# Tile-wise waits between pools, even gate steps, and low one-hot products on GpSimd in a PEER transformer layer

## The chip, the cores and the metric

The kernel runs on one core of a Trainium2 chip. The metric is the device time of one execution in microseconds (us). Before the change three runs took 3026.48, 3026.91 and 3030.73 us; the median is 3026.91. One execution was profiled, and all durations below come from its trace.

The engines are called by the trace's short names too: PE is TensorE (matrix products), DVE is VectorE, ACT is ScalarE, POOL is GpSimd and SP is SyncE, which here only issues DMAs.

## What is computed

The reference is one layer of a diffusion transformer for 1024 tokens of width 1024, with a final norm. First comes a block of windowed attention, a short convolution and a gated merge. Then comes the PEER block, a layer of 16,384 experts, each a vector u and a vector v. Each token picks 16 experts for each of 8 heads:

```
s      = einsum(query, sub_keys)                  # 128 scores for each of 2 key halves
best   = top 16 of (top 16 of s[0]) + (top 16 of s[1])
g      = softmax(best)                            # gates, 8 heads x 16
act    = gelu(u[idx] . token)
out    = sum over the 128 picks of g * act * v[idx]
```

The kernel computes this block in two ways. For the first 512 tokens (the first half, `hf = 0`) and for 384 of the second 512 it takes the dense way: all experts are applied to all tokens as large matrix products, and a gate matrix G (experts x tokens, zero where an expert was not picked) multiplies gelu(u . token) or, for those 384, the stored product. For the second half the values gelu(u . token) come from gathered rows of u, and the last 128 tokens also gather their rows of v.

To keep fp32 accuracy, operands are split into a high and a low fp16 part, and a product is three products: high x high, high x low, low x high.

## The kernel before, in words

The gate matrix is built in tiles of 128 tokens. `select` (line 839) is one tile's top-k work on VectorE. `build_g` (965) then makes G for the tile. It goes through 16 groups of 8 tokens. For each group it makes four tiles of 128x1024 fp16 on VectorE: `e1`, a one-hot of the first expert index; `ah` and `al`, e1 times the high and the low part of the gate; and `e2`, a one-hot of the second index. Each is a product of two tiles in SBUF, with step-0 broadcasts. `expand` (997) multiplies e2 with ah and with al on TensorE into PSUM; ScalarE copies the result to a tile `ge`, and after two groups a DMA stores ge to the DRAM tensor `gd`: from GpSimd's queue in the first half, from ScalarE's in the second. A group is expanded one group after its tiles were made. e1 has one buffer; ah, al and e2 have two. `gates(0)` (1011) runs select and build_g for the four tiles of the first half while `stage2(1)` (718) runs the merge and the query projections of the second half. `gates_stream` (1043) does the same for the second half while the experts run.

Work of two kinds is interleaved when the program is written. `run_side` (1059) takes a main generator (which yields at each step) and a gates generator. After each main step it adds credit for gate steps, `grate` times the TensorE time that a simple model gives to that main step, and takes a gate step for each whole unit of credit. `GATES_B = 0.64` is the rate beside stage2(1), `GATES_D = 0.072` beside the experts. Before tile (1, 0) has been selected, credit is 1 per main step. The gathered rows have a rate of their own. A gates generator that has to wait (for the dot products of its tile) yields False; then the loop ends and the credit stays. When the main steps are over, gate steps that are left run at once. VectorE's order is tied to this order: a gate step's VectorE instructions stand behind the main step's last one. GpSimd and SyncE each run their own instructions in order.

`experts` (1386) drives the dense stage. For the first half there are 128 slots (`slot_dense`, 1158), one for each block of 128 experts: 24 matrix products with u (`ups`), gelu, the gate product, the split into `wdh` and `wdl`, and two of the eight output blocks of the previous group of four slots (`res`, `vps`, 12 products each). 376 main steps make up the first half. The second half (`slot_mix`, 1199) loads gates from gd again (`gt`), and its first load needs all of the second half's gd. Around slot 0 three u products with early weights (`u_first`, made in the pool `wts`) run first, and the slots 0 to 2 read gelu values from DRAM (`gel<-ged`).

Memory is handed out by pools that are opened and closed like a stack on two sides of SBUF. In this kernel a pool that lands on the bytes of closed pools waits, with all its tiles, for every user of those pools. The pools of the dense stage (`acc`, `dense0`, `gate1`, and `psV` in PSUM) are opened after `wts`, `gate0`, both `half` pools, `s2` and `x1` have been closed (lines 1408 to 1475).

Of the kernel before, what the change touches and what calls it, by code (L numbers as in the profile page):

```python
# [11 lines left out]
F16 = mybir.dt.float16  # L12
# [6 lines left out]
PSUM = bass.MemoryType.PSUM  # L19

D = 1024
# [8 lines left out]
TB = 8  # L30
REP = 4
NDENSE = 512
NMIX = 384
LATE_DOTS = 34
GATES_B = 0.64
GATES_D = 0.072
AHEAD = 1
GR = 8
GATE_AT = (2, 5)
# [3 lines left out]
SUB = 4  # L43
# [79 lines left out]
class K:  # L123
# [9 lines left out]
        self.waiting = []  # L133
        self.turned = None

    def pool(self, name, side=None, space=None, bufs=1):
        kw = {}
        if side is not None:
            kw["side"] = side
        if space is not None:  # L140
            kw["space"] = space
        g = self.tc.tile_pool(name=name, bufs=bufs, **kw)
        p = g.__enter__()
        return g, p
# [820 lines left out]
    def build_g(self, t, hf):  # L965

        nc, p = self.nc, self.pg
        yield
        yield
        ii, g16 = self.slots(t, hf)  # L970
        yield
        late = []
        for q in range(128 // 16):
            ge = p.tile([128, 128, 16], F32, name="ge", tag="ge", bufs=self.ge_bufs)
            for sub in range(16 // TB):
                t0 = q * 16 + sub * TB
                ts = slice(t0, t0 + TB)

                def onehot(name, src, idx, op):
                    x = p.tile([128, TB, 128 // REP, REP], F16, name=name, tag=name, bufs=1 if name == "e1" else 2)  # L980
                    nc.vector.tensor_tensor(x, src, idx[:, ts].unsqueeze(2).to_broadcast([128, TB, 128 // REP, REP]),
                                            op=op)
                    return x

                e1 = onehot("e1", self.iota, ii[:, 0], ALU.is_equal)
                ah = onehot("ah", e1, g16[:, 0], ALU.mult)
                al = onehot("al", e1, g16[:, 1], ALU.mult)
                e2 = onehot("e2", self.iota, ii[:, 1], ALU.is_equal)
                late.append((t, hf, q, sub, ge, ah, al, e2))
                if len(late) > 1:  # L990
                    self.expand(*late.pop(0))
                yield
        for x in late:
            self.expand(*x)
            yield
# [20 lines left out]
    def open_gate(self, name, side, ge_bufs):  # L1016
        nc, a = self.nc, self.a
        self.ge_bufs = ge_bufs
        g, self.pg = self.pool(name, side=side)
        p = self.pg  # L1020
        io32 = p.tile([128, 128], F32, name="io32", tag="dot", bufs=1)
        nc.sync.dma_start(io32, a["iota"])
        io16 = p.tile([128, 128], F16, name="iotas")
        nc.vector.tensor_copy(io16, io32)
        self.iota = io16.rearrange("p (a b) -> p a b", b=REP).unsqueeze(1).to_broadcast([128, TB, 128 // REP, REP])
        self.cand = p.tile([128, 8, NCAND], F32, name="cand", tag="cand", bufs=1)
        nc.vector.memset(self.cand[:, :, 16:128], NEG)
        self.iota16 = p.tile([128, 16, 16], F16, name="iota16")
        nc.vector.tensor_copy(self.iota16, io32[:, 0:16].unsqueeze(2).to_broadcast([128, 16, 16]))
        return g  # L1030
# [28 lines left out]
    def run_side(self, main, gates=None, grate=0.0, rows=None, rate=0.0, first=None):  # L1059


        pe, dve = self.nc.tensor, self.nc.vector
        last = pe.spent
        due = gdue = 0.0
        alive = gates is not None
        for _ in main:
            spent = pe.spent - last
            with nullcontext() if dve.pin else self.tc.issue_after(dve.last):
                due += rate
                while due >= 1.0:  # L1070
                    due -= 1.0
                    if next(rows, False) is False:
                        due = 0.0
                gdue += 1.0 if first is not None and first not in self.sel else grate * spent
                while alive and gdue >= 1.0:
                    r = next(gates, StopIteration)
                    alive = r is not StopIteration
                    if r is False:
                        break
                    gdue -= 1.0  # L1080
            last = pe.spent
        if alive:
            for _ in gates:
                pass
# [50 lines left out]
    def split_v(self, i1, v32, p):  # L1135
        if v32 is None:
            return self.vparts[i1]
        vh = p.tile([128, D], F16, name="vh", tag="vh", bufs=2 * SUB)
        vl = p.tile([128, D], F16, name="vl", tag="vl", bufs=2 * SUB)
        self.nc.scalar.activation(vh, v32, AF.Copy, scale=16.0)  # L1140
        self.late[0].append((vl, v32, 16.0, vh))
        if i1 >= 128 - 2 * SUB:
            self.vparts[i1] = vh, vl
        return vh, vl
# [13 lines left out]
    def slot_dense(self, i1, p, pv, outs):  # L1158
        nc = self.nc
        nb = NDENSE // 32  # L1160
        hh, hl = self.h2h[0], self.h2l[0]
        self.load_u(i1 + 2, p)
        v32 = self.load_v(0, i1, p)
        self.block_gates(0, i1, p)
        wh = self.pac.tile([128, NDENSE], F16, name="wdh", tag="wdh", bufs=2 * SUB)
        wl = p.tile([128, NDENSE], F16, name="wdl", tag="wdl", bufs=2 * SUB)
        ge = p.tile([128, NDENSE], F32, name="gel", tag="gel", bufs=2)
        if i1 < UPRE:
            nc.sync.dma_start(ge, self.ged[i1])
        else:  # L1170
            uh, ul = self.uparts.pop(i1)
            ps = pv.tile([128, 512], F32, name="ups", tag="v", bufs=3)
            for k in range(8):
                self.mm3(ps, uh[:, k, :], ul[:, k, :], hh[:, k, :], hl[:, k, :], k == 0, k == 7)
        self.lows(1)
        self.lows(0)
        if outs:
            yield 0
        if i1 >= UPRE:
            nc.scalar.activation(ge, ps, AF.Gelu, scale=2.0 ** -12)  # L1180
        self.split_u(i1 + 2, p)
        vh, vl = self.split_v(i1, v32, p)
        ends = []
        for k, out in enumerate(outs):
            ends.append(out())
            if k == 0:
                yield 0
        for end in ends:
            end()
        gev = ge.rearrange("p (b t) -> p b t", t=16)  # L1190
        for q in range(2):
            qs = slice(nb * q, nb * q + nb)
            nc.vector.tensor_mul(gev[:, qs, :], gev[:, qs, :], self.gts[q][:, :, i1 % GR, :])
        nc.scalar.activation(wh, ge, AF.Copy, scale=256.0)
        self.late[0].insert(0, (wl, ge, 256.0, wh))
        yield 0
        return vh, vl, wh, wl

    def slot_mix(self, i1, p, outs):
        nc = self.nc  # L1200
        nb = NMIX // 32
        v32 = self.load_v(1, i1, p)
        self.block_gates(1, i1, p)
        self.lows(0)
        vh, vl = self.split_v(i1, v32, p)
        wh = self.pac.tile([128, NMIX], F16, name="wdh", tag="wdh", bufs=2 * SUB)
        wl = p.tile([128, NMIX], F16, name="wdl", tag="wdl", bufs=2 * SUB)
        parts = [w.rearrange("p (b t) -> p b t", t=16) for w in (wh, wl)]
        for q in range(2):
            qs = slice(nb * q, nb * q + nb)  # L1210
            g = self.gts[q][:, :, i1 % GR, :]
            nc.scalar.activation(parts[0][:, qs, :], g, AF.Copy, scale=256.0)
            self.late[0].insert(q, (parts[1][:, qs, :], g, 256.0, parts[0][:, qs, :]))
        yield 1
        self.lows(0)
        for out in outs:
            out()()
            yield 1
        return vh, vl, wh, wl
# [188 lines left out]
    def run(self):  # L1408
        nc, a = self.nc, self.a
# [8 lines left out]
        for hf in (1, 0):  # L1418
            g, p = self.pool(f"half{hf}", side="left")
# [39 lines left out]
        self.close(g_pw)  # L1459
        self.close(g_pa)  # L1460
        self.close(g_pf)
        g_pv, pv = self.pool("psV", space=PSUM)
        self.pf, self.ftag = pv, ("v", 3)
        self.bank = self.fbank
        g_ac, self.pac = self.pool("acc", side="left")
        self.part = self.pac.tile([128, 8 - NRES, HALF], F32, name="part")
        gd, pd = self.pool("dense0", side="left")
        g_g = self.open_gate("gate1", "right", 1)
        self.experts(pd, pv)
        self.close(gd)  # L1470
        self.close(g_ac)
        self.close(g_g)
        self.close(g_pv)
        self.close(self.g_pc)
# [63 lines left out]
```

## Time and profile before

| | |
|---|---|
| median of three runs | 3026.91 us |
| the profiled execution | 3026.57 us |
| its span, first to last instruction | 3024.8 us |
| PE busy | 2869.4 us, 95% |
| DVE busy | 2647.7 us, 88% |
| ACT busy | 1174.2 us, 39% |
| POOL busy | 1063.1 us, 35% |
| mean granted TensorE clock | 0.981 of full speed |

A busy share is a mean over stages that differ. The stages follow each other so: attention, convolution and the first merge until about 600 us; the second merge and the queries with the first half's gate tiles until 1084 us; the dense stage from there to the end, with the change from its first to its second half at about 2480 us. In rows of stretches, a figure such as 41.54 (x64) is busy time in us and the count of instructions. In rows of a timeline, the bracket gives how long the engine had stood idle before, and what it had waited for. In rows of groups, the count is followed by the summed busy time and the mean in ns. Instructions of one engine overlap a little, so the next one may start before the sum of start and duration.

### The profile page before, as it was taken

What the parts mean: (1) busy time and instruction counts of PE and PEld (TensorE: products, weight loads), DVE (VectorE), ACT (ScalarE), POOL (GpSimd) and SP (SyncE); (2) the same over time, 40 slices, a digit from 0 to 9 for tenths busy, and PEclk for the clock granted to TensorE, in tenths of its full rate; (3) what the DMA queues carried; (4) which work ended last, traced back from release to release, by engine and by line L of the source; (5) the groups of instructions that cost most, each with busy time, mean ns of one, the idle gap of its engine ahead of it and who ended that gap; (6) DMA issues with size and microseconds to landing.
All of it is one profiled execution on the core that took longest, in us unless ns stands there. A gap on an engine that the chain in (4) does not pass through costs nothing.

```text
span 3024.8 us, 49092 instructions
## 1 busy us (share of the span) xinstructions
PE 2869.4 (95%) x18685; PEld 1527.1 (50%) x18685; DVE 2647.7 (88%) x5438; ACT 1174.2 (39%) x1878; POOL 1063.1 (35%) x814
## 2 busy tenths in 40 slices
PE   6899999989989978999999999999999989999998
PEld 2465555444444433444444444444444446767675
DVE  7788776699999979999899998999979979888887
ACT  4844576423434232233233332333333323433342
POOL 3200012201121004554444444555444435455553
PEclk9999999999999988999999999999999999999999
DMA  6234436654445448899899998999989989999995
GB/s 225 94 116 123 117 125 183 227 169 151 177 167 192 160 154 287 321 334 321 307 321 345 341 345 292 328 328 333 342 318 334 325 294 316 381 366 351 349 365 197
DMA packets 327197, 795.74 MB, mean 263 GB/s; under 512 B 22960, under 2 KB 147248, under 8 KB 319792
## 3 DMA queue, kind: packets, MB, share of 16 engines
q1 hardware_dynamic: 219536, 372.08, 37.1%
q0 software_dynamic: 103968, 395.36, 35.4%
q10 hardware_dynamic: 3456, 25.17, 2.0%
q8 instruction: 146, 2.39, 0.3%
q14 instruction: 91, 0.75, 0.1%
HBM read 696.31 MB, written 96.21 MB: 262 GB/s over the span
## 4 chain that ended last, share of the span: by engine, by line
PE 44%; DVE 16%; issue 6%; POOL 3%; DMA 3%; ACT 1%; SPq 0%; DVEq 0%; POOLq 0%; ACTq 0%
PE res L72 23%; PE ups L72 13%; PE vps L72 5%; DVE row L72 3%; POOL row L917 3%; DMA row<-u,ci 2%; DVE vl L72 1%; PE fbank L72 1%; DVE e L72 1%; DVE eq L72 1%; PE bank L72 1%; DVE ul L72 1%; DVE si L72 1%; DVE wdl L72 1%; DVE sv L72 1%
## 5 line engine op out<-in xcount | busy, mean ns | idle before, releaser
L917 POOL DMA_INDIRECT row<-u,ci x512 | 674.6, 1318 | 899.5 <-DVE row L72 637.7
L72 DVE SCALAR_TENSOR_TENSOR row<-row,hn 128x1024 f32<-128x1024 f32 x512 | 614.6, 1223 | 75.5 <-DMA row<-u,ci 57.9
L72 PEld LDWEIGHTS <-vh 128*128 128x128 f16 x5120 | 469.6, 98 | 357.3 <-issue 24.3
L72 PE MATMUL res<-wdl,vh 128*128 128x128 f16 (+2 forms) x2176 | 628.2, 306 | 13.7 <-DVE wdl L72 13.6
L72 PE MATMUL res<-wdh,vh 128*128 128x128 f16 (+2 forms) x2176 | 625.6, 306 | 12.2 <-ACT wdh L72 12.2
L72 PE MATMUL res<-wdh,vl 128*128 128x128 f16 (+2 forms) x2176 | 625.3, 306 | 4.7 <-DVE vl L72 4.7
L72 PE MATMUL ups<-h,uh 128*128 128x512 f16 x1952 | 582.4, 380 | 0.0
L72 PEld LDWEIGHTS <-whl 128*128 128x128 f16 x3288 | 317.5, 100 | 370.8 <-issue 50.0
L72 PE MATMUL bank<-hT,whl 128*128 128x512 f16 x1584 | 378.7, 388 | 15.4 <-ACT hT L72 6.0
L72 ACT ACTIVATE vh<-v 128x1024 f16<-128x1024 f32 x248 | 260.1, 1049 | 307.1 <-PE res L72 163.0
L72 PE MATMUL ups<-h,ul 128*128 128x512 f16 x976 | 371.3, 380 | 5.6 <-DVE ul L72 5.6
L72 PEld LDWEIGHTS <-vl 128*128 128x128 f16 x2560 | 250.8, 98 | 195.8 <-DVE vl L72 22.9
L72 DVE SCALAR_TENSOR_TENSOR vl<-v,vh 128x1024 f16<-128x1024 f32 x248 | 301.9, 1218 | 10.3 <-ACT vh L72 10.3
L72 PEld LDWEIGHTS <-uh 128*128 128x128 f16 x1952 | 190.9, 98 | 228.7 <-issue 1.9
L917 POOL DMA_INDIRECT row<-v,ci x128 | 217.3, 1698 | 173.6 <-DVE wdl L72 88.6
L72 ACT ACTIVATE gel<-ups 128x512 f32<-128x512 f32 x125 | 74.6, 597 | 403.1 <-PE ups L72 392.2
L72 ACT ACTIVATE wdh<-gel 128x512 f16<-128x512 f32 x128 | 80.5, 629 | 354.1 <-DVE gel L72 338.0
L72 ACT ACTIVATE ge<-fbank 128x512 f32<-128x512 f32 x224 | 121.6, 594 | 222.3 <-PE fbank L72 187.0
L72 DVE SCALAR_TENSOR_TENSOR racc<-row,fig,racc 128x1024 f32<-128x1024 f32 x127 | 162.6, 1281 | 9.3 <-DMA row<-v,ci 7.0
L72 DVE TENSOR_TENSOR e<-iotas,ii 128x1024 f16<-128x1024 f16 x224 | 153.3, 708 | 7.9 <-ACT ii L72 4.8
L72 PEld LDWEIGHTS <-ul 128*128 128x128 f16 x976 | 95.6, 98 | 122.4 <-DVE ul L72 7.0
L72 PE MATMUL vps<-wdh,vh 128*128 128x512 f16 x384 | 145.6, 379 | 5.2 <-ACT ge L72 4.3
(223 smaller groups left out, 4211.4 us busy)
## 6 DMA issues: line engine op xcount, KB each, us to landing
v<-v SPq DMA_DIRECT2D x248, 512.0 KB
u<-u_t SPq DMA_DIRECT2D x122, 512.0 KB
gd<-ge POOLq DMA_DIRECT2D x32, 1024.0 KB
gt<-gd SPq DMA_DIRECT2D x32, 1024.0 KB
wm<-w_mod SPq DMA_DIRECT2D x48, 512.0 KB
gd<-ge ACTq DMA_DIRECT2D x24, 1024.0 KB
gt<-gd SPq DMA_DIRECT2D x32, 768.0 KB
w<-w_in SPq DMA_DIRECT2D x34, 512.0 KB
```

What stands on the lines that cost most here:

```text
L72: r = f(*args, **kw)
L917: self.nc.gpsimd.indirect_dma_start(out=r, out_offset=None, in_=tab, in_offset=bass.IndirectOffsetOnAxis(ap=ci[:, s:s + 1], axis=0))
```

## The change

Three edits are made together.

1. *Pools that wait tile by tile.* `pool` passes options on, and the pools psV, acc, dense0 and both gate pools get `reuse_waits="tile"`: each of their tiles waits only for the users of earlier tiles on its own bytes. vh, vl and wdl move from dense0 to a new pool `parts`, which is opened below acc, so that it lies on the lowest bytes of that side, where `wts` lay.
2. *Even gate steps.* GATES_D goes from 0.072 to 0.085, and when the gates generator has to wait, the credit is cut to at most 1.
3. *Low products on GpSimd.* In the first half's `build_g`, al is made by GpSimd. e1 gets two buffers there, and ah, al and e2 three; a group is expanded two groups after its tiles were made. The second half's build_g is as it was.

```diff
-GATES_D = 0.072
+GATES_D = 0.085
...
-    def pool(self, name, side=None, space=None, bufs=1):
-        kw = {}
+    def pool(self, name, side=None, space=None, bufs=1, **kw):
...
                 def onehot(name, src, idx, op):
-                    x = p.tile([128, TB, 128 // REP, REP], F16, name=name, tag=name, bufs=1 if name == "e1" else 2)
-                    nc.vector.tensor_tensor(x, src, idx[:, ts].unsqueeze(2).to_broadcast([128, TB, 128 // REP, REP]),
-                                            op=op)
+                    x = p.tile([128, TB, 128 // REP, REP], F16, name=name, tag=name,
+                               bufs=(3 if hf == 0 else 2) - (name == "e1"))
+                    eng = nc.gpsimd if name == "al" and hf == 0 else nc.vector
+                    eng.tensor_tensor(x, src, idx[:, ts].unsqueeze(2).to_broadcast([128, TB, 128 // REP, REP]), op=op)
                     return x
...
-                if len(late) > 1:
+                if len(late) > (1 if hf else 2):
                     self.expand(*late.pop(0))
...
     def open_gate(self, name, side, ge_bufs):
-        g, self.pg = self.pool(name, side=side)
+        g, self.pg = self.pool(name, side=side, reuse_waits="tile")
...
                     if r is False:
+                        gdue = min(gdue, 1.0)
                         break
...
     def split_v(self, i1, v32, p):
-        vh = p.tile([128, D], F16, name="vh", tag="vh", bufs=2 * SUB)
-        vl = p.tile([128, D], F16, name="vl", tag="vl", bufs=2 * SUB)
+        vh = self.ppt.tile([128, D], F16, name="vh", tag="vh", bufs=2 * SUB)
+        vl = self.ppt.tile([128, D], F16, name="vl", tag="vl", bufs=2 * SUB)
...
-        wl = p.tile([128, NDENSE], F16, name="wdl", tag="wdl", bufs=2 * SUB)
+        wl = self.ppt.tile([128, NDENSE], F16, name="wdl", tag="wdl", bufs=2 * SUB)
...
-        wl = p.tile([128, NMIX], F16, name="wdl", tag="wdl", bufs=2 * SUB)
+        wl = self.ppt.tile([128, NMIX], F16, name="wdl", tag="wdl", bufs=2 * SUB)
...
-        g_pv, pv = self.pool("psV", space=PSUM)
+        g_pv, pv = self.pool("psV", space=PSUM, reuse_waits="tile")
...
-        g_ac, self.pac = self.pool("acc", side="left")
+        g_pt, self.ppt = self.pool("parts", side="left", reuse_waits="tile")
+        g_ac, self.pac = self.pool("acc", side="left", reuse_waits="tile")
...
-        gd, pd = self.pool("dense0", side="left")
+        gd, pd = self.pool("dense0", side="left", reuse_waits="tile")
...
         self.close(g_ac)
+        self.close(g_pt)
```

## Rows read from the trace of the kernel before

**Rows 1.** The page, part 1: busy us (share of the span), instructions, by engine.
```profile
PE 2869.4 (95%) x18685; PEld 1527.1 (50%) x18685; DVE 2647.7 (88%) x5438; ACT 1174.2 (39%) x1878; POOL 1063.1 (35%) x814
```

**Rows 2.** Busy times by stretch: start:end length, PE PEld DVE ACT POOL, clock, DMA, GB/s.
```profile
1500.00:2450.00 950.00, 940.19 (x4834) 445.57 (x4833) 878.51 (x1467) 321.88 (x441) 453.21 (x341) 1.00 0.92 329
```

**Rows 3.** Busy times by stretch: the first building stretch, and the sum of all four.
```profile
714.00:757.00 43.00, 40.62 (x343) 23.14 (x342) 41.54 (x64) 19.87 (x35) 8.70 (x9) 0.96 0.55 208
sum 174.00, PE 163.53 PEld 94.82 DVE 170.09 ACT 80.88 POOL 33.75; mean PE 40.88 PEld 23.71 DVE 42.52 ACT 20.22 POOL 8.44
```

**Rows 4.** Busy times by stretch: after the gate tiles of the first half.
```profile
1003.00:1084.00 81.00, 72.83 (x466) 37.64 (x466) 81.00 (x496) 19.89 (x34) 0.53 (x1) 0.98 0.27 88
```

**Rows 5.** Groups by line, VectorE, 714 to 1004 us: busy us, mean ns, idle before.
```profile
L72 DVE TENSOR_TENSOR al<-e,g 128x1024 f16<-128x1024 f16 x64 | 45.9, 718 | 0.0
```

**Rows 6.** Timeline of VectorE, 733 to 740 us: start us, us, instruction.
```profile
734.75 0.69 DVE L72 TENSOR_TENSOR ah<-e,g 128x1024 f16<-128x1024 f16 x1
735.36 0.69 DVE L72 TENSOR_TENSOR al<-e,g 128x1024 f16<-128x1024 f16 x1
736.08 1.64 DVE L72 TENSOR_TENSOR e<-iotas,ii 128x1024 f16<-128x1024 f16 x1
738.36 1.65 DVE L72 TENSOR_TENSOR al<-e,g 128x1024 f16<-128x1024 f16 x1
```

**Rows 7.** Groups by line, GpSimd, 400 to 560 us, columns as in rows 5.
```profile
L740 POOL TENSOR_TENSOR sa<-sa,sgv 128x512 f32<-128x512 f32 x6 | 7.6, 1268 | 4.8 <-DVE sgv L72 4.7
L742 POOL TENSOR_TENSOR ml<-sa,mh 128x512 f16<-128x512 f32 x6 | 7.6, 1264 | 3.0 <-ACT mh L72 3.0
```

**Rows 8.** Timeline of GpSimd, 700 to 910 us.
```profile
733.73 3.44 POOL L740 TENSOR_TENSOR sa<-sa,sgv 128x512 f32<-128x512 f32 x1 [1.14 <-DVE sgv L72]
...
766.32 1.26 POOL L740 TENSOR_TENSOR sa<-sa,sgv 128x512 f32<-128x512 f32 x1 [4.61 <-DVE sgv L72]
...
903.88 6.27 POOL L326 TENSOR_TENSOR sq<-sq 128x512 f32<-128x512 f32 x1 [4.91 <-ACT sq L72]
```

**Rows 9.** Timeline of TensorE, start of the dense stage; in brackets idle time and releaser.
```profile
1075.18 17.26 PE L72 MATMUL ups<-h,whl 128*128 128x512 f16 x72 [0.73 <-ACT sl L72]
1104.39 1.01 PE L72 MATMUL res<-wdh,vh 128*128 128x512 f16 x2 [11.95 <-ACT wdh L72]
```

**Rows 10.** Timeline of SyncE's queue, the same place.
```profile
1062.01 0.33 SPq L173 DMA_DIRECT2D w<-u_t  x1
...
1092.47 0.33 SPq L1132 DMA_DIRECT2D v<-v  x1
```

**Rows 11.** Timeline of VectorE, the same place.
```profile
1097.26 1.22 DVE L72 SCALAR_TENSOR_TENSOR vl<-v,vh 128x1024 f16<-128x1024 f32 x1 [10.32 <-ACT vh L72]
1102.92 0.76 DVE L72 TENSOR_TENSOR gel<-gel,gt 128x256 f32<-128x256 f32 x2 [4.44 <-DMA gel<-ged]
```

**Rows 12.** Busy times by stretch: the end of the dense stage's first half.
```profile
2460.00:2465.00 5.00, 3.96 (x37) 2.37 (x34) 4.89 (x10) 2.80 (x5) 1.15 (x1) 1.00 0.74 244
2465.00:2470.00 5.00, 2.10 (x24) 1.77 (x25) 4.79 (x9) 0.00 (x0) 0.00 (x0) 0.76 0.79 308
2470.00:2475.00 5.00, 3.58 (x32) 3.19 (x32) 4.01 (x7) 2.17 (x4) 0.00 (x0) 0.56 0.32 131
2475.00:2480.00 5.00, 2.44 (x13) 1.32 (x13) 0.78 (x2) 2.44 (x5) 0.00 (x0) 0.78 0.88 262
```

**Rows 13.** Timeline of ScalarE and its DMA queue, the same place.
```profile
2470.34 2.29 ACT L72 ACTIVATE ge<-fbank 128x512 f32<-128x512 f32 x4 [5.70 <-DMA gd<-ge]
2476.91 2.08 ACT L72 ACTIVATE ge<-fbank 128x512 f32<-128x512 f32 x4 [4.28 <-DMA gd<-ge]
2479.02 0.33 ACTq L72 DMA_DIRECT2D gd<-ge  x1
2487.78 0.36 ACT L72 ACTIVATE wdh<-gt 128x192 f16<-128x192 f32 x1 [8.03 <-DMA gt<-gd]
```

**Rows 14.** Timeline of SyncE's queue, the same place.
```profile
2483.02 3.83 SPq L1092 DMA_DIRECT2D gt<-gd  x3
```

## The prediction

> **What bounds the kernel now.** I read the page's shares first. TensorE is busy for 95% of the span and VectorE for 88% [rows 1], so the whole kernel is a TensorE kernel, and what an edit is worth depends on the stretch in which it lies. So next I read busy times by stretch. From 1500 to 2450 us TensorE works 940.2 of 950 us [rows 2]: nothing gained on another engine counts there unless VectorE, with 878.5, runs out of room. The first half's gate tiles are built in four stretches (one for each tile of 128 tokens), 174 us together, and there VectorE works 170.1 and TensorE 163.5 [rows 3]: VectorE's order sets the pace, and TensorE is only 10.5 us short of full. From 1003 to 1084 VectorE has no gap at all, from top-k work that the change leaves alone [rows 4]. Then I read the two places where TensorE stands still for long: at the start of the dense stage (one stop of 12 us [rows 9]) and at the end of its first half (2460 to 2480 us [rows 12]).
>
> **1. The low gate tile on GpSimd.** Each of the 64 groups of 8 tokens runs four products of 128x1024 fp16 on VectorE: e1, ah, al, e2. The 64 al tiles are 45.9 us of its busy time [rows 5]. Neighbours overlap a little, so a tile takes 0.61 us of the queue (ah starts at 734.75, al at 735.36 [rows 6]); 64 x 0.61 = 39 us leave VectorE.
>
> What arrives at GpSimd? The trace has no 128x1024 fp16 product there. The nearest rows are 128x512 products: 1268 ns with fp32 all through and 1264 ns with one fp16 input and an fp16 output [rows 7]. Narrower data buys nothing, so the element count sets the time, and I estimate 2 x 1.27 = 2.5 us for an al when nothing disturbs it, 162 us in all. GpSimd has that room on paper.
>
> But such a product isn't undisturbed beside the one-hot products. The product issued at 733.73 took 3.44 us and the one at 903.88 took 6.27 [rows 8]; one that falls among VectorE's top-k instructions took 1.26 (766.32 [rows 8]). And VectorE pays as well: its e at 736.08 took 1.64 us and its al at 738.36 took 1.65, where their neighbours take 0.69 [rows 6]. That is 0.96 us lost to VectorE for each 512-element product of GpSimd. They take turns: GpSimd starves while VectorE streams, and when it gets in, VectorE stands.
>
> Beside these rows stands a rule. The Trainium skill, "SBUF — State Buffer", section "Who interferes with whom", says that a VectorE instruction with two SBUF inputs contends with a GpSimd instruction that reads SBUF, and that whoever is first holds the shared port pair to its end while the other fully blocks. The trace agrees (1.64 against 0.69 us); it shows in addition that being queued first doesn't help GpSimd, which was overtaken for some 5 us at 903.88. The same notes, "GPSIMD Engine Reference", section "Performance versus the Vector engine", give 4497 ns for a two-input fp32 add of 2048 elements; half of it is an estimate of 2.25 us for one al, and with that as the stall for every group the term below would be 64 x (2.25 - 0.61) = +105 us.
>
> My term: an al has twice the elements, so it stops VectorE for 2 x 0.96 = 1.92 us. e1, ah and e2, with nothing between, are three more two-input products of 0.61, so there is no cover for it in a building stretch. Nor can VectorE run away from it: e1 has two buffers, so e1 of group n+2 waits until al of group n has been made. Queued behind that e1 are the stage's own instructions on VectorE (the merges sa and sgv, the sums into x), for which TensorE's next projections wait. Expanding two groups later gives TensorE cover for a late al, but VectorE's total is what bounds, and it becomes 1.92 - 0.61 = 1.31 us longer per group: 64 x 1.31 = +84 us. The last two al of each tile fall into the next selection, where GpSimd's product ran in 1.26 us and so was free: 8 x 1.92 = 15 us back. **Term: +69 us.**
>
> Bounds. Below: no stall at all; then TensorE, which has 10.5 us of idle time in these stretches, is the bound, and the term is -10.5. With the stall of a 512-element product (the same bytes) it is 64 x (0.95 - 0.61) - 8 x 0.95 = +14. Above: each al stops VectorE for the whole 2.56 us and none is hidden: 64 x (2.56 - 0.61) = +125. I take +69, because the pair of rows at 1268 and 1264 ns speaks for elements and against bytes. GpSimd's other instructions stand behind the al tiles in its queue too: sa, ml and sq, and the store of each finished ge. sa and ml are needed only when all eight column blocks are merged; the store is covered by the second ge buffer. I cost them at nothing; without that cover, a store that comes late makes ScalarE wait for its ge buffer and then TensorE.
>
> **2. Pools that wait tile by tile.** Before, SyncE's last weight load goes at 1062.01 and the first v load of the dense stage at 1092.47 [rows 10], in the moment that the three early u products end (1075.18 + 17.26 = 1092.44 [rows 9]): their weight tiles lie in a closed pool whose bytes the dense pools take over, and the load waits for all users of it. Then vl starts at 1097.26 and the gating at 1102.92 [rows 11], and TensorE stands for 11.95 us until 1104.39 [rows 9]. With waits by tile, v32, gt and gel lie on bytes whose users are long done, so these loads can go more than 20 us earlier. What still lies on the weight tiles' bytes is the new pool of vh, vl and wdl, so a first vh or wdl may wait for one of the three u products. VectorE is free from 1084, so the first gating and vl run beside the u products, and TensorE goes on at about 1094. **Term: -10 us** (bounds: 0, if what is late next is vh, and -12, the whole stop). The shorter stops of TensorE that follow come from VectorE's order (a selection in a burst, then the first gathered rows) and move along with it. The second gate pool's loads go earlier too, but VectorE, which would use them, is in its top-k work until 1084 [rows 4].
>
> **3. Even gate steps.** In the dense stage gate steps are paid from TensorE's modelled time: a slot is 24 + 24 products of 512 columns, 48 x 512 / 2370 = 10.37 us, so 0.072 x 10.37 = 0.75 steps for each slot. Counting the 376 steps of the first half so (12 of them one by one until the first selection, and a wait for each tile's dots), 103 of the 108 gate steps have been issued when the half ends, and five are run out at once. That is what the trace shows: four groups in a row with one ge buffer, ScalarE waiting 5.70 and 4.28 us for the store of the previous ge [rows 13], and TensorE idle for 1.04 + 2.90 + 1.42 + 2.56 = 7.9 us [rows 12]; the second half's first gt load goes only at 2483.02 [rows 14]. At 0.085 the same count issues all 108, the last at step 373. The cap on the credit keeps steps that were blocked from coming in a heap. The stores and the gt load (here 2479.02 to 2483.02 and on to 2487.78, 4.0 and 4.8 us [rows 13, 14]) then fit under the outputs of the last group, 8 x 2.59 = 20.7 us of TensorE. **Term: -8 us** (bounds: 0 and -8). The steps come 18% closer together, in stretches where VectorE has 950 - 878.5 = 71 us to spare; I cost this at nothing, and without that cover a few us come back.
>
> **Sum.** 69 - 10 - 8 = +51 us on the profiled execution's 3026.57 us (span 3024.8; the median of the runs is 3026.91, so nothing is to be converted): **3078 us**. Own range of this case: 3045 to 3115.
>
> **Rivals.**
> A. The two engines do run side by side, and al is simply off VectorE's path. For it: GpSimd is nearly empty there (33.8 us busy of 174 [rows 3]), and tiles in threes give it two groups of slack. Against it: every one-hot product in these stretches reads two SBUF tiles like those that lost 0.96 us. The gain ends where TensorE is full: -10.5 - 10 - 8 gives 2998 us. This is the other side. It decides at a stall of 0.61 us an al: below that, VectorE gains.
> B. The stall goes by bytes: +14 - 18 = -4, 3023 us, no change to be seen.
> C. An al holds VectorE for its whole time and nothing hides it: +125 - 18 = +107, 3134 us.
> D. The tile waits do nothing, because SyncE's queue meets another late user ahead of the v load: 10 us more in any case above. It stays inside their ranges.
>
> **How the numbers follow.** Forecast 0.60, A 0.25, B 0.09, C 0.06. A measurement of this kernel can tell about 0.2% (6 us) from no change. Faster: A and a little of B, 0.27. Within: most of B and an edge of the others, 0.07. Slower: 0.66. The range from 2988 to 3130 leaves out the lower edge of A and most of C.
>
> **What would show it.** In the after trace: al on GpSimd at 2 us or more with a wide spread; one-hot products on VectorE of 2 to 2.7 us, or VectorE waiting for al before e1, and the four building stretches at 55 to 65 us each instead of 43. If these stay at 43 us or less, the main term is wrong, and A holds. TensorE's stop after the early u products should shrink from 12 us to 2 or less, with v loads issued before 1092 us on this clock; at the end of the first half, no two groups back to back and no idle slice of more than 1 us.

## The result, and the profile after

The changed kernel takes 3071.66 us (median of 4 runs, 3067.81 to 3072.03) against 3026.69 us of the kernel before (4 runs beside them): ratio 1.0148, 95% interval 1.0135 to 1.0162, 45 us slower. 3078 was forecast, in a range of 2988 to 3130.

The page's busy row, which answers to [rows 1]: GpSimd has 132 us more, VectorE 62 us more although 64 products left it.

```profile
PE 2872.2 (94%) x18685; PEld 1532.8 (50%) x18685; DVE 2710.0 (88%) x5374; ACT 1175.4 (38%) x1878; POOL 1195.3 (39%) x878
```

Groups of instructions by line, 600 to 1150 us (busy us, mean ns of one, idle time before them), the answer to [rows 5]. In the same view of the kernel before, ah takes 45.1 us in all (mean 705 ns) and e 87.8 (726).

```profile
L982 POOL TENSOR_TENSOR al<-e,g 128x1024 f16<-128x1024 f16 x64 | 146.6, 2293 | 115.9 <-DVE e L72 53.1 <-DVE g L72 45.8 <-PE fbank L72 15.3
L72 DVE TENSOR_TENSOR ah<-e,g 128x1024 f16<-128x1024 f16 x64 | 123.6, 1935 | 0.3
L72 DVE TENSOR_TENSOR e<-iotas,ii 128x1024 f16<-128x1024 f16 x128 | 111.7, 908 | 7.4 <-ACT ii L72 6.2 <-POOL al L982 1.2
```

The timeline of VectorE in the first building stretch (start us, us, instruction):

```profile
717.41 2.38 DVE L72 TENSOR_TENSOR ah<-e,g 128x1024 f16<-128x1024 f16 x1
719.72 1.28 DVE L72 TENSOR_TENSOR e<-iotas,ii 128x1024 f16<-128x1024 f16 x2
720.92 2.38 DVE L72 TENSOR_TENSOR ah<-e,g 128x1024 f16<-128x1024 f16 x1
723.23 1.28 DVE L72 TENSOR_TENSOR e<-iotas,ii 128x1024 f16<-128x1024 f16 x2
```

And that of GpSimd in the same microseconds, to be read beside it:

```profile
716.97 2.28 POOL L982 TENSOR_TENSOR al<-e,g 128x1024 f16<-128x1024 f16 x1 [1.23 <-DVE e L72]
720.48 2.28 POOL L982 TENSOR_TENSOR al<-e,g 128x1024 f16<-128x1024 f16 x1 [1.23 <-DVE e L72]
724.06 2.21 POOL L982 TENSOR_TENSOR al<-e,g 128x1024 f16<-128x1024 f16 x1 [0.77 <-PE fbank L72]
```

GpSimd starts al as soon as e1 is there, at 716.97, and works until 719.25. The ah issued on VectorE at 717.41 ends at 719.79, 0.54 us after that: it has done its work only behind al. A group with nothing between its products takes 3.51 us (717.41 to 720.92, three products on VectorE) where the same group of the kernel before took 2.44 us (four times 0.61).

Busy times by stretch, columns as in [rows 2]: the first building stretch, over the same length as in [rows 3] and to its end.

```profile
714.00:757.00 43.00, 27.03 (x221) 15.21 (x219) 42.97 (x36) 12.53 (x23) 31.13 (x18) 0.87 0.35 135
712.00:768.50 56.50, 40.46 (x323) 22.90 (x322) 56.31 (x49) 19.34 (x35) 39.73 (x23) 0.88 0.38 149
```

VectorE still has no gap, but in 43 us it gets through 36 instructions instead of 64, and TensorE falls from 40.6 us of work to 27.0.

The start of the dense stage, timeline of SyncE's queue, answering to [rows 10]:

```profile
1081.89 0.38 SPq L1133 DMA_DIRECT2D v<-v  x1
1084.05 0.37 SPq L1093 DMA_DIRECT2D gt<-gd  x1
...
1090.67 3.53 SPq L1170 DMA_DIRECT2D gel<-ged  x1
```

TensorE there, answering to [rows 9]:

```profile
1147.10 15.70 PE L72 MATMUL ups<-h,whl 128*128 128x512 f16 x72
1163.59 0.38 PE L72 MATMUL res<-wdl,vh 128*128 128x512 f16 x1 [0.57 <-DVE wdl L72]
```

The v load now goes 65 us ahead of the early u products (before, 17 us behind their start), and the stop of 11.95 us behind them is gone. The end of the dense stage's first half, busy times by stretch as in [rows 12], the slice with TensorE's least work:

```profile
2515.00:2520.00 5.00, 4.76 (x35) 2.63 (x34) 2.47 (x4) 2.03 (x4) 3.79 (x3) 1.00 0.96 338
```

The timeline of ScalarE and its DMA queue there, as in [rows 13]:

```profile
2518.68 0.33 ACTq L72 DMA_DIRECT2D gd<-ge  x1
2533.00 0.36 ACT L72 ACTIVATE wdh<-gt 128x192 f16<-128x192 f32 x1 [9.66 <-DMA gt<-gd]
```

This slice lacks 0.24 us of TensorE, where four of before lacked 7.9 us together. Against the kernel before, the last expand product of the gate tiles starts 72.9 us later (1076.6 against 1003.7), the first product of res 58.3 (1162.64 against 1104.39), the last split u product (an `ups` of a slot, with u in its two fp16 parts, unlike the three early ones) 60.1 (2516.7 against 2456.6), and the wdh of the second half that waits for the gt load 45.2 (2533.00 against 2487.78). So the loss is made before 1077 us, and won back in part at the two places of parts 2 and 3.

### The profile page after: what moved, and what is told of

Same layout as the page of the kernel before. It is cut to its first block, busy times and chain, and to the rows that moved or that the text cites. A ratio compares the mean times of both kernels' runs of the same rounds, so it can differ in the third digit from the quotient of the medians.

```text
span 3069.4 us, 49152 instructions
## 1 busy us (share of the span) xinstructions
PE 2872.2 (94%) x18685; PEld 1532.8 (50%) x18685; DVE 2710.0 (88%) x5374; ACT 1175.4 (38%) x1878; POOL 1195.3 (39%) x878
## 4 chain that ended last, share of the span: by engine, by line
PE 34%; issue 11%; DVE 11%; POOL 6%; DMA 4%; ACT 0%; POOLq 0%; SPq 0%; DVEq 0%; ACTq 0%
PE res L72 20%; PE ups L72 8%; POOL row L916 6%; PE vps L72 3%; DVE row L72 3%; DMA row<-u,ci 3%; PE bank L72 2%; DVE vl L72 1%; PE fbank L72 1%; DVE ul L72 1%; DVE eq L72 1%; DVE wdl L72 1%; DVE gel L72 1%; DVE e L72 0%; DVE part L72 0%
## 5 line engine op out<-in xcount | busy, mean ns | idle before, releaser
L982 POOL TENSOR_TENSOR al<-e,g 128x1024 f16<-128x1024 f16 x64 | 146.6, 2293 | 115.9 <-DVE e L72 53.1
L72 PE MATMUL fbank<-ah,e 128*128 128x128 f16 x896 | 124.9, 227 | 67.6 <-DVE ah L72 55.2
L72 DVE TENSOR_TENSOR e<-iotas,ii 128x1024 f16<-128x1024 f16 x224 | 177.4, 812 | 7.4 <-ACT ii L72 6.2
L72 PEld LDWEIGHTS <-e 128*128 128x128 f16 x1792 | 115.6, 102 | 117.3 <-DVE ah L72 73.1
```

The costliest lines, as they stand in the source:

```text
L72: r = f(*args, **kw)
L982: eng.tensor_tensor(x, src, idx[:, ts].unsqueeze(2).to_broadcast([128, TB, 128 // REP, REP]), op=op)
```

## The experiments

### The parts one by one

All four ran on one chip beside the kernel before (3025.28 us, 11 runs).

**Al back on VectorE** (parts 2 and 3 of the prediction alone): the changed kernel with
```diff
-                    eng = nc.gpsimd if name == "al" and hf == 0 else nc.vector
+                    eng = nc.vector
-                               bufs=(3 if hf == 0 else 2) - (name == "e1"))
+                               bufs=2 - (name == "e1"))
-                if len(late) > (1 if hf else 2):
+                if len(late) > 1:
```


> The changed kernel with its third part undone: al on VectorE again, the buffers of before, expanded one group later. Parts 1 and 2 stay. Theory (GpSimd's low products and VectorE's one-hot products take turns, which cost 73 us up to the end of the gate tiles): the last expansion ends near 1004 us on the trace again and the kernel takes 3027 - 14 - 6 - 15 + 8 = about 2999 us (2990 to 3008). Rival A (the products run side by side, and something else in the change is slow): undoing it gains nothing, 3065 us or more. Rival E (the tile waits are what delays the stage): also 3065 or more.

Measured: 3000.51 us, ratio 0.9918 (0.9904 to 0.9933). Undoing one part of the change turns it from 45 us slower to 25 us faster; the part costs 1.0148 / 0.9918 = 1.023 (1.021 to 1.025), 71 us. The last expand product starts at 997.6 us.

**Al on GpSimd alone**: the reverse of that diff, on the kernel before.

> The kernel before with the third part alone: al of the first half on GpSimd, e1 in two buffers, ah, al and e2 in three, expanded two groups later. Theory: the gate tiles end 73 us later and nothing gives it back, 3100 us (3092 to 3106). Rival A: no slower than before. Rival E: about 3027.

Measured: 3103.32 us, ratio 1.0252 (1.0233 to 1.0271), +78 us.

**Tile waits alone**: the kernel before with `reuse_waits="tile"` in the same pools and the new pool of vh, vl and wdl.

> The kernel before with the first part alone: pools that wait tile by tile, and the pool of vh, vl and wdl. Theory (the traces before and after show 13.6 us less at the first output product and 20.8 us less at the first split u product): TensorE's stop of 12 us behind the early u products goes, 3027 - 14 to -20, so 3007 to 3013 us. My term on record was -10 (3017). Rival (SyncE's queue holds the loads all the same): 3027.

Measured: 3014.45 us, ratio 0.9961 (0.9947 to 0.9976), -10.8 us. TensorE's stop is gone (its timeline):
```profile
1075.08 18.01 PE L72 MATMUL ups<-h,whl 128*128 128x512 f16 x72
1093.87 0.38 PE L72 MATMUL res<-wdl,vh 128*128 128x512 f16 x1 [0.57 <-DVE wdl L72]
```

The heap at the end of the half is still there (ScalarE's timeline):

```profile
2458.19 1.57 ACT L72 ACTIVATE ge<-fbank 128x512 f32<-128x512 f32 x3 [4.81 <-DMA gd<-ge]
...
2464.57 2.29 ACT L72 ACTIVATE ge<-fbank 128x512 f32<-128x512 f32 x4 [3.96 <-DMA gd<-ge]
```

The first output product comes 11.5 us earlier (1092.92 against 1104.39) and the last split u product 11.3 us (2445.3 against 2456.6). The first split u product comes 17.6 us earlier (1103.0 against 1120.6), but not for a longer gain: 37 output products stand ahead of it where 59 stood before, and the other 22 (0.216 us each, 4.8 us) now run behind it.

**Even gate steps alone**: the kernel before with
```diff
-GATES_D = 0.072
+GATES_D = 0.085
                     if r is False:
+                        gdue = min(gdue, 1.0)
                         break
```


> The kernel before with the second part alone: GATES_D at 0.085 and the credit cut to 1. Theory: the stop at the end of the first half goes, 8 to 15 us, and the denser gate steps give back up to 8 us in the dense stage: 3014 to 3022 us. Rival (the denser steps cost nothing, and the 8 us lost in the dense stage of the changed kernel come from elsewhere): 3012. Rival (no gain left after the give-back): 3027.

Measured: 3009.99 us, ratio 0.9945 (0.9929 to 0.9961), -15.3 us, below the theory's interval: the rival with no price for closer steps. The stop at the start stays (TensorE's timeline):
```profile
1100.55 1.01 PE L72 MATMUL res<-wdh,vh 128*128 128x512 f16 x2 [12.21 <-ACT wdh L72]
```

The waits for a ge store at the end are gone (ScalarE's timeline):

```profile
2458.22 1.09 ACT L72 ACTIVATE ge<-fbank 128x512 f32<-128x512 f32 x2 [4.52 <-PE fbank L72]
2459.34 0.33 ACTq L72 DMA_DIRECT2D gd<-ge  x1
```

The single parts add up to 78 - 10.8 - 15.3 = +52 us; together they cost 45. Each of these differences is known to some 4 to 6 us, so the 7 us between them are not clear of noise.

### What it is in the GpSimd product that costs

These four ran on another chip (before: 3025.50 us, 9 runs); each is the changed kernel with one edit.

**The later expansion without GpSimd**: `eng = nc.vector` for al, the extra buffers and the two-group delay kept.

> The changed kernel with the low products al back on VectorE, but with the extra buffers of the one-hot tiles and the expansion two groups later, as the change has them. Theory (the cost is the GpSimd product and what it does to VectorE's product beside it, 3071.7 against 3000.5 us with al on VectorE): buffers and a later expansion cost nothing by themselves, 2996 to 3006 us, the last gate product of the first half near 998 us, ah near 0.70 us. Rival (the later expansion itself moves gate products past the due times of the selection stage and carries part of the 71 us): 3015 us or more, the last gate product after 1010 us.

Measured: 3009.32 us, ratio 0.9944 (0.9927 to 0.9961). It falls between the two: the delay may not be quite free (8.8 us over al on VectorE with the old depth, with intervals that overlap a little; the last expand product starts at 1013.9, after 1010 as the rival had it), but 62 of the 71 us come from GpSimd. What the delay costs VectorE is seen in its idle time ahead of e, 16.8 us where the old depth has 5.8, most of it waiting for TensorE:
```profile
L72 DVE TENSOR_TENSOR e<-iotas,ii 128x1024 f16<-128x1024 f16 x128 | 82.8, 684 | 16.8 <-PE fbank L72 12.3 <-ACT ii L72 4.4
```

**GpSimd only writes**:
```diff
+                    if name == "al" and hf == 0:
+                        nc.gpsimd.memset(x, 0.0)
+                        return x
-                    eng = nc.gpsimd if name == "al" and hf == 0 else nc.vector
+                    eng = nc.vector
```


> The changed kernel, but GpSimd fills al with zeros by a memset and reads neither the one-hot tile nor the gate; the low gate parts of the first half are so left out of its result. Theory (the two engines stop each other over what they read: 64 stalls of 1.70 us, 2.38 - 0.68, each beside a product that reads two tiles): ah falls from 1.94 us on average to 0.65 to 0.85 us, and the time to 2990 to 3010 us. Rival 1 (any GpSimd instruction that touches the memory holds VectorE's fast 16-bit products until it ends): ah is longer than its 0.70 us by about the memset's own length, and with a memset of 1 us, say, 64 x 1 = 64 us at most, 3040 to 3065 us. Rival 2 (what costs is the wait of TensorE for al through GpSimd's queue, not VectorE): ah short and the time still above 3040 us.

Measured: 2971.29 us, ratio 0.9819 (0.9803 to 0.9836), 19 us below the theory's interval. Groups by line:
```profile
L982 POOL MEMSET al<- 128x1024 f16 x61 | 57.8, 959 | 81.2 <-PE fbank L72 81.0
L72 DVE TENSOR_TENSOR ah<-e,g 128x1024 f16<-128x1024 f16 x64 | 43.5, 680 | 0.0
```

The timeline of GpSimd:

```profile
717.24 0.95 POOL L982 MEMSET al<- 128x1024 f16 x1 [0.85 <-PE fbank L72]
```

And that of VectorE:

```profile
717.18 0.68 DVE L72 TENSOR_TENSOR ah<-e,g 128x1024 f16<-128x1024 f16 x1
717.78 1.28 DVE L72 TENSOR_TENSOR e<-iotas,ii 128x1024 f16<-128x1024 f16 x2
```

A write of a whole al by GpSimd lies right beside ah, and ah takes its 0.68 us. This ah starts 0.06 us ahead of the write, but the first of the two e behind it starts in the middle of it, and the two take 1.28 us, as elsewhere. That al and ah read the same e1 isn't the cause: in the kernel before, sa on GpSimd shares no tile with the e beside it, and that e too ends 0.55 us after sa (737.72 against 737.17 [rows 6, 8]). So neither GpSimd's writing nor its queue holds VectorE; it is its reading. This is what the Trainium skill states ("SBUF — State Buffer", section "Who interferes with whom"): a VectorE instruction with two SBUF inputs contends with a GpSimd instruction that reads SBUF, and not with one that only writes it; the trace agrees, 0.68 us beside the memset and 2.38 beside the product.

**GpSimd reads one tile**: in place of the memset, `nc.gpsimd.tensor_copy(x, src)`.

> The changed kernel, but GpSimd makes al as a copy of the one-hot tile: it reads one tile where the product reads two; the low gate parts of the first half are so replaced by ones, and its result is not the reference's. Theory (the stall comes with GpSimd's second read stream, or lasts as long as the GpSimd instruction): if it lasts as long as the instruction, ah is near 0.70 us plus the copy's length less what of it ran ahead; with a copy of 1.1 to 1.5 us that is 64 x (1.0 - 0.6) = 26 us to 64 x (1.4 - 0.6) = 51 us over 3000 us, 3025 to 3050 us. If only a GpSimd instruction with two inputs stops VectorE: ah near 0.70 us and 2995 to 3010 us. Rival (any GpSimd instruction of 1024 elements takes its 2.2 us and costs the same): 3065 to 3075 us.

Measured: 3015.41 us, ratio 0.9970 (0.9957 to 0.9982), 6 us over the run with the delay alone, between the first two intervals that were written down. Groups by line:
```profile
L982 POOL COPY al<-e 128x1024 f16<-128x1024 f16 x64 | 91.2, 1428 | 116.6 <-DVE e L72 99.7 <-PE fbank L72 15.6 <-PE bank L72 1.3
L72 DVE TENSOR_TENSOR ah<-e,g 128x1024 f16<-128x1024 f16 x64 | 84.9, 1330 | 0.3
```

The timeline of GpSimd:

```profile
716.68 1.44 POOL L982 COPY al<-e 128x1024 f16<-128x1024 f16 x1 [1.21 <-DVE e L72]
```

And that of VectorE:

```profile
717.14 1.52 DVE L72 TENSOR_TENSOR ah<-e,g 128x1024 f16<-128x1024 f16 x1
718.58 1.28 DVE L72 TENSOR_TENSOR e<-iotas,ii 128x1024 f16<-128x1024 f16 x2
```

Again ah ends 0.54 us after GpSimd's instruction (718.66 against 718.12). One input is enough for the stall, and it lasts as long as GpSimd still works: 0.84 us (1.52 - 0.68) beside a copy of 1.44, 1.70 (2.38 - 0.68) beside a product of 2.28. The expectation missed because it took a stall of 1.0 to 1.4 us. On average a group's ah is longer by 1.33 - 0.70 = 0.63 us and its two e by 0.21 (96.0 us against 82.8 with the later expansion alone, over 64 groups), 0.84 together, where al itself had taken 0.61 of VectorE's queue; and VectorE waits 10 us less ahead of e (6.5 against 16.8).

**Every second al on GpSimd**: `hf == 0 and sub` in the choice of the engine.

> The changed kernel with al on GpSimd in every second group only (32 of 64). Theory (each al on GpSimd costs the path the same 71 / 64 = 1.1 us): 3000.5 + 32 x 1.1 = 3036 us, 3028 to 3044; ah comes in two sorts, near 0.70 and near 2.38 us. Rival (VectorE has slack in the selection stage that takes up a smaller load, so that the first offloads are free): 3000 to 3015 us. Second rival (one late al delays both of its neighbours in TensorE's order): 3050 us or more.

Measured: 3043.97 us, ratio 1.0068 (1.0047 to 1.0088): 35 us over the run with the delay alone, 43 over that with the old depth, at the upper edge of the first interval. Half of the products cost 35 of 62 us or 43 of 71, a little over half; there is no slack that takes up the first ones.

### Depth, and another engine

On a third chip (before: 3023.76 us, 9 runs).

**Al on GpSimd with the old depth**: the changed kernel with the old buffers and one group of delay.

> The changed kernel with al on GpSimd, but with the buffers and the one-group delay of the kernel before (the counterpart of the run with the later expansion alone). Theory (a group takes 3.5 us with al on GpSimd, and al is done 2.3 us after its one-hot tile, so one group ahead is enough, and the later expansion hides nothing; by itself it even cost 9 us, 3009.3 against 3000.5): 3060 to 3073 us. Rival (the later expansion does hide al's latency, as GpSimd also carries gate stores and starts al late): TensorE waits for al in most groups, 3080 us or more.

Measured: 3075.79 us, ratio 1.0162 (1.0148 to 1.0177), between the two intervals and not to be told from the change (1.0148). Neither theory nor rival gives the whole of it: here ah averages 1.02 us, but e takes 1.24, VectorE waits 16.1 us for al to release the only e1 buffer, and TensorE 36.3 us for al:
```profile
L72 DVE TENSOR_TENSOR e<-iotas,ii 128x1024 f16<-128x1024 f16 x128 | 155.8, 1241 | 24.0 <-POOL al L982 16.1 <-ACT ii L72 5.9 <-PE fbank L72 1.5
L72 PE MATMUL fbank<-al,e 128*128 128x128 f16 x512 | 67.0, 228 | 36.3 <-POOL al L982 36.3
```

So the depth does hide al from TensorE (36.3 us of waits become 7.4 in the changed kernel), but VectorE's products and waits add up to the same in both (245.8 and 243.0 us in the table below), and so does the time.

**Every second al on ScalarE**, on the run with al back on VectorE:
```diff
+                if hf or not sub:
                     al = onehot("al", e1, g16[:, 1], ALU.mult)
+                else:
+                    al = p.tile([128, TB, 128 // REP, REP], F16, name="al", tag="al", bufs=2)
+                    for u in range(TB):
+                        nc.scalar.activation(al[:, u].rearrange("p a b -> p (a b)"),
+                                             e1[:, u].rearrange("p a b -> p (a b)"), AF.Copy,
+                                             scale=g32[:, t0 + u:t0 + u + 1])
```
(g32 is a float32 copy of the low gate part, one for each 128 tokens.)

> The changed kernel with the old depth, and al on VectorE in every first group, on ScalarE in every second (eight activations of 128x128 each, scaled by a column of the gate in float32, with one more small copy on VectorE per 128 slots). Theory (in this stage the end follows VectorE's busy time one to one: against the run with the later expansion alone, 40.5 us less of it gave 38.0 us less of time, and 62.9 us more gave 62.4 us more): 32 products of 0.70 us leave VectorE, 22 us, and four copies of some 0.1 to 0.2 us come: 3000.5 - 21.5 = 2979 us, 2974 to 2986; ah stays near 0.70 us, since ScalarE does not stop VectorE as GpSimd does. Rival 1 (ScalarE does so too): ah longer than 1 us in every second group, 2990 us or more. Rival 2 (the evictions of the gate tiles on ScalarE come late behind eight small activations, and TensorE waits for them): ah short, waits of TensorE for ge up by 10 us or more, 2985 to 3005 us.

Measured: 3001.47 us, ratio 0.9922 (0.9907 to 0.9938): nothing gained over al on VectorE, where 2974 to 2986 was expected. The ah stays at 0.69 us, so ScalarE doesn't stop VectorE, but eight activations take 2.44 us and hold the only e1 buffer meanwhile; the wait moved there:
```profile
L72 DVE TENSOR_TENSOR e<-iotas,ii 128x1024 f16<-128x1024 f16 x128 | 90.3, 735 | 24.1 <-ACT al L72 17.1 <-ACT ii L72 6.3 <-PE fbank L72 0.5
L72 DVE TENSOR_TENSOR ah<-e,g 128x1024 f16<-128x1024 f16 x64 | 43.9, 686 | 0.7
```

**The same with two buffers of e1** in the first half (`bufs=2 - (name == "e1" and hf == 1)`, and the float32 copy made in the first half alone), on a fourth chip (before: 3027.13 us, 7 runs):

> The run before with al of every second group on ScalarE, and the first one-hot tile e1 in two buffers in the first half (in that run VectorE stood 17.1 us in 15 waits for ScalarE's al to release the only e1 buffer). Theory (those waits took back what the offload gave): they go, VectorE's busy time of the stage is 22 us under that of the run with al on VectorE, and the time is 3000.5 - 15 to 22 us: 2978 to 2986 us. Rival (something else bounds the stage as soon as VectorE is ahead: the evictions on ScalarE, or the due times of the gate steps): 2993 us or more, with VectorE idle elsewhere in the stage.

Measured: 2989.11 us, ratio 0.9872 (0.9855 to 0.9889), faster than both kernels, 38 us under the kernel before and some 82 under the changed one, and between the theory and the rival. It is 11 us better than al on VectorE (14 by the ratios), half of what the offload takes off VectorE: the waits for ScalarE's al are gone, and in their place VectorE waits before ah for TensorE to release the buffers of an older group.
```profile
L72 DVE TENSOR_TENSOR e<-iotas,ii 128x1024 f16<-128x1024 f16 x128 | 84.0, 695 | 7.6 <-ACT ii L72 7.4 <-PE fbank L72 0.2
L72 DVE TENSOR_TENSOR ah<-e,g 128x1024 f16<-128x1024 f16 x64 | 46.2, 723 | 15.0 <-PE fbank L72 14.6
```

### One table over them

All kernels here have the tile waits and the even steps. For each: VectorE's busy time on e, ah and al from 600 to 1150 us, its idle time ahead of them (both from the groups by line of the profiled run), their sum, and the median time. The profiled run's own time lies up to 8 us off that median.

| al of the first half | e + ah + al | idle | sum | time |
|---|---|---|---|---|
| written by GpSimd, no read | 131.9 | 6.0 | 137.9 | 2971.3 |
| half on ScalarE, two e1 | 152.2 | 22.6 | 174.8 | 2989.1 |
| half on ScalarE, one e1 | 158.0 | 24.8 | 182.8 | 3001.5 |
| VectorE, old depth | 177.7 | 6.3 | 184.0 | 3000.5 |
| copied by GpSimd | 180.9 | 6.8 | 187.7 | 3015.4 |
| VectorE, later expansion | 172.4 | 16.8 | 189.2 | 3009.3 |
| half on GpSimd | 198.0 | 16.2 | 214.2 | 3044.0 |
| GpSimd, as changed | 235.3 | 7.7 | 243.0 | 3071.7 |
| GpSimd, old depth | 220.8 | 25.0 | 245.8 | 3075.8 |

From the first row to the last the sum grows by 108 us and the time by 104; time less sum stays between 2814 and 2834 in all nine. So over the whole span what VectorE's products and waits take in this stage is paid nearly in full, whichever engine is to blame. Step by step it isn't exact: from the first row to the second the sum grows by 37 us and the time by 18. In the first row VectorE waits 25.4 us for TensorE's products ahead of the stage's own instructions (sa, sgv and x), in the second 3.3, and the sum leaves these waits out.

## Why the prediction was right, step by step

**What bounds.** Right. In the building stretches VectorE's order sets the pace, and the table shows it over a span of 108 us. What was wrong is the floor of rival A: "the gain ends where TensorE is full", 10.5 us. With al off VectorE and no stall, the time fell by 29 us against al on VectorE with the old depth, to 2971 instead of rival A's 2998, and the three early u products started at 1050.3 us instead of 1071.0. Not all of TensorE's work in these stretches is bound to them: they were 30 us shorter (140.5 against 170.9 from the first ah to the last, all four) and held 133.9 us of TensorE's work instead of 159.5, and the intervals between them were 13 us longer (124.8 against 111.6; the later expansion alone makes them 122.5). A busy share of a stretch is no floor for it when the engine has other work there that can move. A floor there is, only lower: the 25.4 us that VectorE then waits for TensorE point to it.

**Al on GpSimd, +69.** Measured +78 alone and +71 within the change; 72.9 us by the start of the last expand product. The path is the forecast one: from 700 us to there TensorE waits 55.2 us for ah and 7.4 for al (before, to 1004 us, 7.2 and 2.1). GpSimd's other instructions, costed at nothing, cost nothing that can be seen (ScalarE waits 26.5 us for sa, before 27.2). The mechanism is the forecast one, turns over reads, and the element count set al's time: 2.2 to 2.3 us typically, where 2.5 was estimated. But that the size came out is luck in part: two errors stand against each other. The four stretches from the first ah to the last grew from 173.7 to 235.0 us, 61 us where 84 were forecast: the stall is 1.70 us in a typical group, not 1.92 (al starts about 0.44 us ahead of ah, and that part stops nobody). And the 15 us that were to hide in the selections between them did not come back: the three intervals between them (last ah of a tile to the first of the next) grew from 112.9 to 124.6 us. The run with the later expansion alone has 122.5 us there, with al on VectorE, so most of that growth belongs to the later expansion, which the prediction held to be cover without a price.

**The bounds.** The starvation that [rows 8] had shown, 6.27 us for one instruction, came only a few times: one al took 7.08 us and two 4.51. Mostly al is issued right behind e1, ahead of ah, and so is first.

**Tile waits, -10.** Right in size (-10.8 alone) and in its reason: the stop of 11.95 us goes, the first output product comes 11.5 us earlier, and at the last split u product 11.3 of them are still there. Nothing is given back on the way that can be seen: from the first split u product to the last TensorE waits 22.1 us for wdl, ul and vl in the kernel before, 23.3 with the tile waits alone and 22.8 in the changed kernel.

**Even steps, -8.** Too small: -15.3 alone. The term counted TensorE's idle slices (7.9 us) and left out two things. One is the clock: behind the first of these idle times the granted clock fell to 0.76, 0.56 and 0.78 [rows 12], where with the even steps it stays at 1.00 (the upper of its two levels) through the same place. From the last split u product to the end of the last group's outputs TensorE takes 38.5 us in the kernel before and 22.1 with this part alone. Of the 16.4 us, 7.7 are idle time; 80 expand products of 0.055 us, 4.4 us, only run earlier, inside the half; some 4 us are left for the slower clock, an estimate by difference. The other is nothing that the edit explains: 3.8 us are won already at the first split u product (1116.8 against 1120.6), ahead of the stretch in which it works; what they come from is open. That the closer steps cost nothing was right: from the first split u product to the last it takes 1340.6 us with them and 1336.0 before, and the 80 expand products that have moved there are 4.4 of these 4.6 us.

**The sum, +51.** Measured +45. The parts alone give +52, and the 7 us between them are within the noise. Of the three terms, al and the tile waits came out near their size, and the even steps at nearly twice theirs.

## What to carry to other kernels

Before a product with two inputs goes to GpSimd, look what VectorE does beside it: if that reads two tiles of the on-chip memory as well, the two don't overlap, and the offload is worth it only if GpSimd's time, less its head start, is shorter than what VectorE saves. Work for GpSimd to be put beside such products is work that only writes; for the rest ScalarE is the engine to try, with a second buffer for the tile that it reads. And when a stage is bound by one engine's order, sum up that engine's busy time and its waits in the stage over several versions: here that one number, with one constant fitted to all of them, gave the time of nine kernels within 10 us.

## What the runs showed of the hardware

- An fp16 product of 128x1024 mostly takes 2.20 to 2.34 us on GpSimd beside VectorE's products (0.69 on VectorE), a copy of that size 1.36 to 1.44, a memset 0.95.
- A VectorE product with two inputs that starts while such a product or copy runs on GpSimd ends 0.54 us after it, at both lengths; beside the memset it takes its own 0.68 us. Between GpSimd reading one tile and two, these rows show no other difference than its length.
- GpSimd, when its instruction is issued first, keeps its pace: 2.28 us at 716.97 with an ah waiting through most of it, no more than twice the 512-element product of [rows 7].
- Eight ScalarE activations of 128x128 beside VectorE's products (2.44 us in all) leave them at 0.69 us.
- With TensorE waiting for one-hot tiles, its granted clock was 0.87 from 714 to 757 us (0.96 before), and its 128x128 expand products averaged 233 ns where al on VectorE gave 220.
